# A DMA-bound 2x2 average pooling: loop bodies of two tiles and two result buffers instead of four, a split first load and a split last store

## The chip, the cores and the metric

One core of a Trainium2 chip. The time is the device time of one execution in microseconds (us); a kernel's figure is the median of several executions. A profiled execution also gives a span (first to last instruction), which in these runs is about 1.8 to 2.0 us shorter than the time of the same execution. The clock column is 1.000 and plays no part: there is no matrix work.

## The reference

```python
x = np.random.randn(32, 128, 256, 256).astype(np.float32)   # n, c, h, w
# kernel_size 2, stride 2
output[:, :, i, j] = np.mean(x[:, :, 2*i:2*i+2, 2*j:2*j+2], axis=(2, 3))
```

1073.74 MB are read and 268.44 MB are written, all in float32, with three additions and one multiplication for each result.

## The kernel before

A "unit" is 128 output rows, one for each partition. A tile has 32 units: 64 KB of input and 16 KB of output in each partition, so 8.39 MB in and 2.10 MB out. There are 127 whole tiles; the last 32 units go through in parts of 16, 8, 4 and 4 units, so that the end is short. SyncE (SP) issues the loads into two input buffers; VectorE (DVE) adds the two rows (first sum, in place) and then neighbouring columns (second sum, into a result buffer); ScalarE (ACT) multiplies by 0.25 and issues the store. SP, ACT and DVE synchronise by hand through semaphores; `take` waits for a semaphore and takes the count away again.

```python
OUTS = 4
ins = [in_pool.tile([P, TILE, 2 * w], f32, name="in_tile") for _ in range(2)]
res = [out_pool.tile([P, TILE, w_out], f32, name="res") for _ in range(OUTS)]

def tile_load(t, b):
    sp.dma_start(out=ins[b], in_=xt[t]).then_inc(loaded[b], 16)

def tile_sum(b, o, first=False):
    it, dst = ins[b], res[o]
    take(dve, loaded[b], 16)
    dve.tensor_add(out=it[:, :, 0:w], in0=it[:, :, 0:w], in1=it[:, :, w:]).then_inc(ready)
    if not first:
        take(dve, stored[o], 16)          # the result buffer's old store, between the sums
    take(dve, ready)
    dve.tensor_add(out=dst, in0=it[:, :, 0:w:2], in1=it[:, :, 1:w:2]).then_inc(summed)

def tile_scale(b, o, done):
    take(act, summed)
    act.sem_inc(free[b])                  # SP may now load into ins[b]
    act.mul(out=res[o], in_=res[o], mul=0.25).then_inc(done)
# ... (tile_store, the parts, the loops over OUTS tiles)
```

## Time and profile before

| | |
|---|---|
| median of 6 executions | 3103.94 us (3103.81 to 3104.12) |
| the profiled execution | 3104.85 us, span 3103.1 us |
| DVE busy, ACT busy | 54%, 15% |
| mean rate of the DMA engines | 433 GB/s |

The page of before: its first and second parts (busy us and share by engine; the span in 40 slices, where a digit is the busy share in tenths), then the DMA queues. Queue q1 holds the loads and q10 the stores; the last column is the time of their packets as a share of 16 DMA engines' span.

```profile
DVE 1679.7 (54%) x262; ACT 464.8 (15%) x132; POOL 0.2 (0%) x4
...
DMA  9999999999999999999999999999999999999999
...
q1 hardware_dynamic: 19008, 1075.85, 80.1%
q10 hardware_dynamic: 18720, 266.35, 20.0%
```

80.1 and 20.0 leave nothing: the DMA engines are the bound. The rhythm is in the timeline of before (columns: start us, length us, engine, line, operation, what it writes and reads, idle time before it and what ended it; SPq and ACTq lines are issues of DMAs by that engine's sequencer):

```profile
1495.40 8.69 DVE L88 TENSOR_TENSOR in_tile<-in_tile 128x8192 f32<-128x8192 f32 x1 [10.91 <-DVEq L70]
1504.24 4.42 DVE L92 TENSOR_TENSOR res<-in_tile 128x4096 f32<-128x4096 f32 x1
1508.86 3.62 ACT L97 ACTIVATE res<-res 128x4096 f32<-128x4096 f32 x1 [20.55 <-ACTq L70]
...
1512.72 0.34 ACTq L101 DMA_DIRECT2D out_dram<-res  x1
1519.59 8.69 DVE L88 TENSOR_TENSOR in_tile<-in_tile 128x8192 f32<-128x8192 f32 x1 [10.93 <-DVEq L70]
```

One tile every 24.18 us; the DVE works 13.1 us of it and waits 10.9 us. "DVEq L70" is the wait inside `take`; it does not tell which semaphore was waited for, so that has to be read from the moments at which DMAs land. The page's part on DMA issues gives the median time from issue to landing (last column):

```profile
out_dram<-res ACTq DMA_DIRECT2D x126, 2048.0 KB, 33.9
in_tile<-in_x_dram SPq DMA_DIRECT2D x127, 34.6
```

Each of these is longer than the 24.18 us period, so in both queues a DMA stands behind its predecessor. The records of single packets show how they share an engine: one 64 KB load packet (2.42 us), one 16 KB store packet (0.61 us), eight such pairs a tile. The chain of waits is of no use here: it ends after two pieces of 0.7 us at the last ScalarE instruction, because the DMAs behind it are not followed.

### The profile page before, as it was taken

What the parts mean: (1) busy time and instruction counts of PE and PEld (TensorE: products, weight loads), DVE (VectorE), ACT (ScalarE), POOL (GpSimd) and SP (SyncE); (2) the same over time, 40 slices, a digit from 0 to 9 for tenths busy, and PEclk for the clock granted to TensorE, in tenths of its full rate; (3) what the DMA queues carried; (4) which work ended last, traced back from release to release, by engine and by line L of the source; (5) the groups of instructions that cost most, each with busy time, mean ns of one, the idle gap of its engine ahead of it and who ended that gap; (6) DMA issues with size and microseconds to landing.
All of it is one profiled execution on the core that took longest, in us unless ns stands there. A gap on an engine that the chain in (4) does not pass through costs nothing. (4 is left out here: it accounts for less than half of the span.)

```text
span 3103.1 us, 2444 instructions
## 1 busy us (share of the span) xinstructions
DVE 1679.7 (54%) x262; ACT 464.8 (15%) x132; POOL 0.2 (0%) x4
## 2 busy tenths in 40 slices
DVE  4555555555555555555555555555555555555555
ACT  1111111111111111111111111111111111111111
POOL 0000000000000000000000000000000000000000
DMA  9999999999999999999999999999999999999999
GB/s 415 436 439 426 436 439 426 436 439 426 436 438 426 436 438 426 436 430 435 436 438 426 440 435 426 436 438 427 436 438 426 437 439 425 437 438 426 437 438 401
DMA packets 37730, 1342.21 MB, mean 433 GB/s; under 512 B 4192, under 2 KB 4192, under 8 KB 4576
## 3 DMA queue, kind: packets, MB, share of 16 engines
q1 hardware_dynamic: 19008, 1075.85, 80.1%
q10 hardware_dynamic: 18720, 266.35, 20.0%
q14 instruction: 2, 0.02, 0.0%
HBM read 1073.74 MB, written 268.44 MB: 433 GB/s over the span
## 5 line engine op out<-in xcount | busy, mean ns | idle before, releaser
L88 DVE TENSOR_TENSOR in_tile<-in_tile 128x8192 f32<-128x8192 f32 x127 | 1104.0, 8693 | 1395.9 <-DVEq L70 1395.9
L97 ACT ACTIVATE res<-res 128x4096 f32<-128x4096 f32 x127 | 459.2, 3616 | 2587.2 <-ACTq L70 2587.2
L92 DVE TENSOR_TENSOR res<-in_tile 128x4096 f32<-128x4096 f32 x127 | 562.0, 4425 | 18.6
L145 DVE TENSOR_TENSOR in_tile<-in_tile 128x1024 f32<-128x1024 f32 (+2 forms) x4 | 9.1, 2287 | 1.3 <-DVEq L70 1.3
L97 ACT ACT_TABLE_LOAD x1 | 1.3, 1283 | 36.5 <-ACTq L70 36.5
L164 ACT ACTIVATE res<-res 128x512 f32<-128x512 f32 (+2 forms) x4 | 4.2, 1056 | 8.4 <-ACTq L70 8.4
L147 DVE TENSOR_TENSOR res<-in_tile 128x512 f32<-128x512 f32 (+2 forms) x4 | 4.9, 1225 | 0.6
L249 POOL MEMSET const-bfloat16-1.0<- 128x1 bf16 x1 | 0.1, 101 | 0.0
L249 POOL MEMSET const-uint8-127<- 128x1 uint8 x1 | 0.1, 101 | 0.0
L249 POOL MEMSET const-float32-0.0<- 128x1 f32 x1 | 0.1, 98 | 0.2 <-issue 0.2
L249 POOL MEMSET const-float32-1.0<- 128x1 f32 x1 | 0.1, 98 | 0.0
## 6 DMA issues: line engine op xcount, KB each, us to landing
out_dram<-res ACTq DMA_DIRECT2D x126, 2048.0 KB, 33.9
in_tile<-in_x_dram SPq DMA_DIRECT2D x1, 4096.0 KB, 25.1
in_tile<-in_x_dram SPq DMA_DIRECT2D x1, 2048.0 KB, 30.2
in_tile<-in_x_dram SPq DMA_DIRECT2D x2, 1024.0 KB, 33.2
out_dram<-res SPq DMA_DIRECT2D x1, 2048.0 KB, 13.8
in_tile<-in_x_dram SPq DMA_DIRECT2D x127, 34.6
out_dram<-res ACTq DMA_DIRECT2D x1, 1024.0 KB, 7.4
out_dram<-res ACTq DMA_DIRECT2D x1, 512.0 KB, 5.4
```

The source lines that it names most:

```text
L88: dve.tensor_add(out=it[:, :, 0:w], in0=it[:, :, 0:w], in1=it[:, :, w:]).then_inc(ready)
L92: dve.tensor_add(out=dst, in0=it[:, :, 0:w:2], in1=it[:, :, 1:w:2]).then_inc(summed)
L97: act.mul(out=res[o], in_=res[o], mul=0.25).then_inc(done)
L145: dve.tensor_add(out=it[:, a:b, 0:w], in0=it[:, a:b, 0:w], in1=it[:, a:b, w:]).then_inc(ready)
L147: dve.tensor_add(out=dst[:, a:b], in0=it[:, a:b, 0:w:2], in1=it[:, a:b, 1:w:2]).then_inc(summed)
L164: act.mul(out=dst[:, a:b], in_=dst[:, a:b], mul=0.25).then_inc(scaled)
L249: nc = _bacc.Bacc("TRN2", target_bir_lowering=False, num_devices=1)
```

## The change

The intent: shorter programs (loop bodies of two tiles instead of four), result buffers in step with the two input buffers plus one for the last parts, an earlier start of the first load, and an earlier end of the last store. Core of the diff:

```diff
-    out_pool = ctx.enter_context(tc.tile_pool(name="outp", bufs=OUTS))      # OUTS = 4
+    out_pool = ctx.enter_context(tc.tile_pool(name="outp", bufs=3))
@@ first load
-        for b in range(2):
-            tile_load(b, b)
+        for p in (slice(0, P, 4), slice(1, P, 2), slice(2, P, 4)):
+            sp.dma_start(out=ins[0][p], in_=xt[0][p]).then_inc(first, 16)
+        load(1, 1)
@@ sums: the store's wait comes before the first sum now, and is for tile t-2
-        take(dve, loaded[b], 16)
-        dve.tensor_add(...).then_inc(ready)            # first sum
-        if not first:
-            take(dve, stored[o], 16)
-        take(dve, ready)
+    def tile_sums(b):
+        take(dve, stored[b], 16)
+        take(dve, loaded[b], 16)
+        sums(ins[b], res[b])                           # both sums
@@ DVE's start
+        for b in range(2):
+            dve.sem_inc(stored[b], 16)
+        take(dve, first, 48)
+        dve.sem_inc(loaded[0], 16)
@@ last 4 units
+                scale(dst[:, a:b], ended)
+                for k, engine in enumerate((act, sp)):
+                    engine.wait_ge(ended, 1)
+                    engine.dma_start(out=to[k::2], in_=dst[k::2, a:b]).then_inc(tail, 16)
# ... (loops, semaphores and names that follow from these are cut)
```

More of the change, by code (lines that the diff above doesn't have):

```diff
@@ L37 @@
 TILE = 32
-OUTS = 4
 def _pool_2x2(ctx, tc, x, out, units):
@@ L52, in _pool_2x2, with sem @@
     in_pool = ctx.enter_context(tc.tile_pool(name="inp", bufs=2))
-    out_pool = ctx.enter_context(tc.tile_pool(name="outp", bufs=OUTS))
+    out_pool = ctx.enter_context(tc.tile_pool(name="outp", bufs=3))
     ins = [in_pool.tile([P, TILE, 2 * w], f32, name="in_tile") for _ in range(2)]
-    res = [out_pool.tile([P, TILE, w_out], f32, name="res") for _ in range(OUTS)]
-    loaded = [ctx.enter_context(nc.semaphore(f"loaded{b}")) for b in range(2)]
-    free = [ctx.enter_context(nc.semaphore(f"free{b}")) for b in range(2)]
-    summed = ctx.enter_context(nc.semaphore("summed"))
-    scaled = ctx.enter_context(nc.semaphore("scaled"))
-    stored = [ctx.enter_context(nc.semaphore(f"stored{b}")) for b in range(OUTS)]
-    tail = ctx.enter_context(nc.semaphore("tail"))
-    ready = ctx.enter_context(nc.semaphore("ready"))
-    held = ctx.enter_context(nc.semaphore("held"))
+    res = [out_pool.tile([P, TILE, w_out], f32, name="res") for _ in range(3)]
+    def sem(name):
+        return ctx.enter_context(nc.semaphore(name))
+    first = sem("first")
+    loaded, free, stored = [[sem(f"{n}{b}") for b in range(2)] for n in ("loaded", "free", "stored")]
+    halfway, summed, scaled, held, ended, tail = [
+        sem(n) for n in ("halfway", "summed", "scaled", "held", "ended", "tail")
+    ]
     def take(engine, sem, n=1):
@@ L79, in _pool_2x2 @@
     ot = ov[0:whole * TILE * P].rearrange("(t p g) f -> t p g f", p=P, g=TILE)
-    loops, left = divmod(whole - OUTS, OUTS)
-    def tile_load(t, b):
-        sp.dma_start(out=ins[b], in_=xt[t]).then_inc(loaded[b], 16)
-    def tile_sum(b, o, first=False):
-        it, dst = ins[b], res[o]
-        take(dve, loaded[b], 16)
-        dve.tensor_add(out=it[:, :, 0:w], in0=it[:, :, 0:w], in1=it[:, :, w:]).then_inc(ready)
-        if not first:
-            take(dve, stored[o], 16)
-        take(dve, ready)
-        dve.tensor_add(out=dst, in0=it[:, :, 0:w:2], in1=it[:, :, 1:w:2]).then_inc(summed)
-    def tile_scale(b, o, done):
-        take(act, summed)
-        act.sem_inc(free[b])
-        act.mul(out=res[o], in_=res[o], mul=0.25).then_inc(done)
-    def tile_store(t, o):
-        take(act, scaled)
-        act.dma_start(out=ot[t], in_=res[o]).then_inc(stored[o], 16)
     parts, a = [], 0
@@ L105, in _pool_2x2, with load, sums @@
         b = rest if rest - a <= 4 else a + (rest - a) // 2
-        parts.append((a, b))
+        parts.append((a, b, sem(f"part{len(parts)}")))
         a = b
-    psem = [ctx.enter_context(nc.semaphore(f"part{k}")) for k in range(len(parts))]
-    with tc.tile_critical():
-        for b in range(2):
-            tile_load(b, b)
-        with sp.Fori(2, 2 + 2 * ((whole - 2) // 2), 2) as i:
+    def load(t, b):
+        sp.dma_start(out=ins[b], in_=xt[t]).then_inc(loaded[b], 16)
+    def sums(it, dst):
+        dve.tensor_add(out=it[:, :, 0:w], in0=it[:, :, 0:w], in1=it[:, :, w:]).then_inc(halfway)
+        take(dve, halfway)
+        dve.tensor_add(out=dst, in0=it[:, :, 0:w:2], in1=it[:, :, 1:w:2]).then_inc(summed)
@@ new lines, in tile_sums, with scale, scale_store @@
+    def tile_sums(b):
+        take(dve, stored[b], 16)
+        take(dve, loaded[b], 16)
+        sums(ins[b], res[b])
+    def scale(dst, done=scaled):
+        act.mul(out=dst, in_=dst, mul=0.25).then_inc(done)
+    def scale_store(t, b, landed):
+        take(act, summed)
+        act.sem_inc(free[b])
+        scale(res[b])
+        take(act, scaled)
+        act.dma_start(out=ot[t], in_=res[b]).then_inc(landed, 16)
+    with tc.tile_critical():
+        for p in (slice(0, P, 4), slice(1, P, 2), slice(2, P, 4)):
+            sp.dma_start(out=ins[0][p], in_=xt[0][p]).then_inc(first, 16)
+        load(1, 1)
+        pairs = (whole - 2) // 2
+        with sp.Fori(2, 2 + 2 * pairs, 2) as i:
@@ L116, in _pool_2x2 @@
             for b in range(2):
                 take(sp, free[b])
-                tile_load(i + b, b)
-        t = 2 + 2 * ((whole - 2) // 2)
-        while t < whole:
+                load(i + b, b)
+        for t in range(2 + 2 * pairs, whole):
             take(sp, free[t % 2])
-            tile_load(t, t % 2)
-            t += 1
+            load(t, t % 2)
         take(sp, free[whole % 2])
-        it, dst = ins[whole % 2], res[whole % OUTS]
-        for (a, b), s in zip(parts, psem):
-            sp.dma_start(out=it[:, a:b], in_=block((whole * TILE + a) * P, b - a)[0]).then_inc(s, 16)
+        it, dst = ins[whole % 2], res[2]
@@ L131, in _pool_2x2 @@
+        for a, b, part in parts:
+            sp.dma_start(out=it[:, a:b], in_=block((whole * TILE + a) * P, b - a)[0]).then_inc(part, 16)
         take(sp, held)
-        sp.dma_start(out=ot[whole - 1], in_=res[(whole - 1) % OUTS]).then_inc(stored[(whole - 1) % OUTS], 16)
-        for o in range(OUTS):
-            tile_sum(o % 2, o, first=True)
-        with dve.Fori(0, loops) as i:
-            for o in range(OUTS):
-                tile_sum(o % 2, o)
-        for o in range(left):
-            tile_sum(o % 2, o)
@@ L142, in _pool_2x2 @@
-        take(dve, stored[whole % OUTS], 16)
-        for (a, b), s in zip(parts, psem):
-            take(dve, s, 16)
-            dve.tensor_add(out=it[:, a:b, 0:w], in0=it[:, a:b, 0:w], in1=it[:, a:b, w:]).then_inc(ready)
-            take(dve, ready)
-            dve.tensor_add(out=dst[:, a:b], in0=it[:, a:b, 0:w:2], in1=it[:, a:b, 1:w:2]).then_inc(summed)
-        for t in range(OUTS):
-            tile_scale(t % 2, t, scaled)
-            tile_store(t, t)
-        with act.Fori(OUTS, OUTS + loops * OUTS, OUTS) as i:
-            for o in range(OUTS):
-                tile_scale(o % 2, o, scaled)
-                tile_store(i + o, o)
@@ L157, in _pool_2x2 @@
-        for t in range(OUTS + loops * OUTS, whole):
-            tile_scale(t % 2, t % OUTS, scaled if t < whole - 1 else held)
-            if t < whole - 1:
-                tile_store(t, t % OUTS)
-        act.sem_inc(free[(whole + 1) % 2], -1)
-        for a, b in parts:
-            take(act, summed)
-            act.mul(out=dst[:, a:b], in_=dst[:, a:b], mul=0.25).then_inc(scaled)
-            take(act, scaled)
-            act.dma_start(out=block((whole * TILE + a) * P, b - a)[1], in_=dst[:, a:b]).then_inc(tail, 16)
@@ L169, in _pool_2x2 @@
-        take(sp, tail, 16 * len(parts))
-        for o in range(OUTS):
-            if o != whole % OUTS:
-                take(sp, stored[o], 16)
+        sp.dma_start(out=ot[whole - 1], in_=res[(whole - 1) % 2]).then_inc(tail, 16)
+        for b in range(2):
+            dve.sem_inc(stored[b], 16)
+        take(dve, first, 48)
+        dve.sem_inc(loaded[0], 16)
+        with dve.Fori(0, whole // 2):
+            for b in range(2):
+                tile_sums(b)
+        if whole % 2:
+            tile_sums(0)
@@ new lines, in _pool_2x2 @@
+        for a, b, part in parts:
+            take(dve, part, 16)
+            sums(it[:, a:b], dst[:, a:b])
+        scale_store(0, 0, stored[0])
+        pairs = (whole - 3) // 2
+        with act.Fori(1, 1 + 2 * pairs, 2) as i:
+            for b in (1, 0):
+                scale_store(i + 1 - b, b, stored[b])
+        for t in range(1 + 2 * pairs, whole - 1):
+            scale_store(t, t % 2, stored[t % 2] if t < whole - 2 else tail)
+        take(act, summed)
+        scale(res[(whole - 1) % 2], held)
@@ new lines, in _pool_2x2 @@
+        for a, b, _ in parts:
+            take(act, summed)
+            to = block((whole * TILE + a) * P, b - a)[1]
+            if b < rest:
+                scale(dst[:, a:b])
+                take(act, scaled)
+                act.dma_start(out=to, in_=dst[:, a:b]).then_inc(tail, 16)
+            else:
+                scale(dst[:, a:b], ended)
+                for k, engine in enumerate((act, sp)):
+                    engine.wait_ge(ended, 1)
+                    engine.dma_start(out=to[k::2], in_=dst[k::2, a:b]).then_inc(tail, 16)
@@ L175, in _generic_pool @@
+        take(sp, tail, 16 * (len(parts) + 3))
+        sp.sem_inc(ended, -1)
 def _generic_pool(ctx, tc, x, out, k, s, n, c, h, w, h_out, w_out):
```

## The prediction

> **What bounds it now.** The DMA engines. The page's slices show them at least 90% busy in all 40; the load queue has 80.1%, the store queue 20.0% of 16 engines' span. In the timeline the first sums of consecutive tiles start every 24.18 us (1495.40, 1519.59). A tile moves 8.39 MB in and 2.10 MB out: 434 GB/s. The Trainium skill, "DMA: Bandwidth & Descriptors", section "Where 436 GB/s comes from", gives 435 as the ceiling; this trace agrees. Its section "Queues, rings and completion order" says each DMA engine takes its queues in turn by packet; the packet records agree: a 64 KB load packet (2.42 us), then a 16 KB store packet (0.61 us), eight pairs a tile, 24.2 us. VectorE is 54% busy (13.1 us a tile), ScalarE 15%: off the path until the tail. From the first packet (1.98 us) to the last the packet records show next to no idle, so three things can move: the head, one straggling DMA engine, the tail.
>
> The straggler: in the landings of every load from 66 us on, 15 engines finish within 0.6 us (66.19 to 66.82) and one 1.8 us later (68.59). It fell behind between 44 and 65 us, during the first store, and never catches up; most engines stop near 3099.2, the last at 3101.5.
>
> **What changes.**
> 1. Two result buffers instead of four, and the store of tile t-2 is awaited before tile t's first sum, not its second. In before, that store lands about 3.0 us after tile t's load (71.61 against 68.59). So each tile's sums start about 3 us later; the wait before them grows from 10.9 us once, but the period stays: the next load is now issued about 16.5 us after the last landing, and the DMA engines work on the load before it for 24.2 us. Some 4 to 8 us of slack remain. Steady state: 0 us.
> 2. First tile as 32+64+32 partitions, all still over 16 engines. In before the engines' first packets start over 1.98 to 2.96 us; a small first DMA should narrow that. Two more issues (0.33 us each) hide behind two packets of 2.4 us. Estimate: 0.3 us gained, up to 0.7. A different start might also spare the straggler: up to -1.8 us, chance about 40%.
> 3. Tail. With the straggler, the 3 us shift reaches tile 126: its sums end near 3083.6 instead of 3080.4; the parts then run back to back on VectorE, about 1.9 us later than before, so the last store is issued near 3098.9 instead of 3097.0, and DMA engines wait for it. Halving it over two queues shortens its start by an estimated 0.3 to 0.5 us (128 packets took 1 us to start on all engines). It lands near 3101.6, as before (3101.81). Without the straggler there is no shift and the end comes near 3100.
> 4. Shorter loops: fewer instructions, none on the path.
>
> **Prediction: 3102.8 us** (-0.03%), range 3099.8 to 3105.5. Faster by over 2%: 0.5%; within 2%: 99%; slower: 0.5%.
>
> **What would show it.** Period between first sums still 24.18 us; DMA 9 in all slices; the wait before a first sum ended by a store's landing, not a load's; first packets' starts less spread; the last landing's distance from the other 15 (1.8 us kept, or gone); last store issue at 3097 to 3099.
>
> **What would make it wrong.** If a load is issued after its predecessor has drained, DMA idles each tile: a period of 25 us costs 100 us (3%). If the split start makes more engines straggle, the end comes 2 to 4 us later.

## The result, and the profile after

| | before | after |
|---|---|---|
| median of 6 executions | 3103.94 us | 3104.09 us (3103.08 to 3104.27) |
| span of the profiled execution | 3103.1 us | 3102.3 us |
| ratio | | 1.0, 95% interval 0.9987 to 1.0013 |

A ratio is the mean time of one kernel's runs over that of the other's of the same rounds, so it is not quite the ratio of the medians quoted. The 0.8 us between the two spans is not a gain: the profiled execution of before took 3104.85 us, 0.9 us above its median.

The page after, the same parts:

```profile
DVE 1679.6 (54%) x262; ACT 464.7 (15%) x132; POOL 0.2 (0%) x4
...
DMA  9999999999999999999999999999999999999999
...
q1 hardware_dynamic: 19120, 1075.98, 80.1%
q10 hardware_dynamic: 18656, 266.22, 20.0%
```

The timeline of after:

```profile
1497.45 8.69 DVE L90 TENSOR_TENSOR in_tile<-in_tile 128x8192 f32<-128x8192 f32 x1 [10.91 <-DVEq L70]
1506.29 4.43 DVE L92 TENSOR_TENSOR res<-in_tile 128x4096 f32<-128x4096 f32 x1
1510.90 3.62 ACT L100 ACTIVATE res<-res 128x4096 f32<-128x4096 f32 x1 [20.56 <-ACTq L70]
...
1514.75 0.34 ACTq L107 DMA_DIRECT2D out_dram<-res  x1
1521.65 8.69 DVE L90 TENSOR_TENSOR in_tile<-in_tile 128x8192 f32<-128x8192 f32 x1 [10.94 <-DVEq L70]
```

And its DMA issues:

```profile
out_dram<-res ACTq DMA_DIRECT2D x126, 2048.0 KB, 30.8
in_tile<-in_x_dram SPq DMA_DIRECT2D x129, 31.5
```

The period is still 24.2 us and each wait is still 10.9 us long; only what ends it is another (a store's landing, not a load's). What moved is in the last two lines: loads and stores land 31.5 and 30.8 us after their issue instead of 34.6 and 33.9. They do not run faster. They are issued 3.1 us later in the same rhythm, because the sums of a tile begin when the store of the tile before last has landed. The start shows it: the third tile's load has landed at 66.80 us, the first tile's store at 69.77 us, and the third tile's first sum starts at 70.02 us (in before it started at 68.72 us, with its load landed at 68.59 us and the store at 71.61 us). The third tile's first sum in before:

```profile
68.72 8.69 DVE L88 TENSOR_TENSOR in_tile<-in_tile 128x8192 f32<-128x8192 f32 x1 [13.04 <-DVEq L70]
```

and in after, with the issue of the next load:

```profile
70.02 8.69 DVE L90 TENSOR_TENSOR in_tile<-in_tile 128x8192 f32<-128x8192 f32 x1 [14.06 <-DVEq L70]
...
83.63 0.33 SPq L87 DMA_DIRECT2D in_tile<-in_x_dram  x1
```

So the change spends 3 us of slack in each tile, and no time.

That left three questions: how much slack there was and is, what the head and the tail gained, and whether the change did anything to the one straggling DMA engine that the prediction read from the profile of before.

### The profile page after: what moved, and what is told of

Read it like the earlier page. It is cut to its first block, busy times and chain, and to the rows that moved or that the text cites. A ratio compares the mean times of both kernels' runs of the same rounds, so it can differ in the third digit from the quotient of the medians.

```text
span 3102.3 us, 2619 instructions
## 1 busy us (share of the span) xinstructions
DVE 1679.6 (54%) x262; ACT 464.7 (15%) x132; POOL 0.2 (0%) x4
## 5 line engine op out<-in xcount | busy, mean ns | idle before, releaser
L90 DVE TENSOR_TENSOR in_tile<-in_tile 128x8192 f32<-128x8192 f32 (+1 forms) x131 | 1113.1, 8497 | 1397.0 <-DVEq L70 1397.0
L100 ACT ACTIVATE res<-res 128x4096 f32<-128x4096 f32 (+1 forms) x131 | 463.5, 3538 | 2594.7 <-ACTq L70 2594.7
L92 DVE TENSOR_TENSOR res<-in_tile 128x4096 f32<-128x4096 f32 (+1 forms) x131 | 566.9, 4327 | 19.2
## 6 DMA issues: line engine op xcount, KB each, us to landing
out_dram<-res ACTq DMA_DIRECT2D x126, 2048.0 KB, 30.8
in_tile<-in_x_dram SPq DMA_DIRECT2D x129, 31.5
```

Of the source, the lines that this page charges most:

```text
L100: act.mul(out=dst, in_=dst, mul=0.25).then_inc(done)
```

## The experiments

Twelve kernels, each correct, in three groups, each run beside before on one chip (two chips in all). Times are medians; ratios are to runs of before on the same chip.

### Was the straggler the kernel's? (before_again, before_split_first, after_whole_first)

**before_again**: no edit.

> A control: the kernel before, unchanged. Theory (the straggling DMA engine comes from how the first tile's packets start, and is there in each execution): in every load from the third on one engine lands 1.5 to 2 us after the other 15. Rival (it is chance of one execution): the lag is another size here, or absent. Time 3103.8 to 3104.2 us.

Measured: 3104.08 us, before 3104.01 us in the same rounds; span 3102.2 us.

**before_split_first**: before with the first load of the changed kernel.

```diff
-        for b in range(2):
-            tile_load(b, b)
+        for p in (slice(0, P, 4), slice(1, P, 2), slice(2, P, 4)):
+            sp.dma_start(out=ins[0][p], in_=xt[0][p]).then_inc(first, 16)
+        tile_load(1, 1)
@@ DVE
+        take(dve, first, 48)
+        dve.sem_inc(loaded[0], 16)
```

> The kernel before with only the first load split in 32, 64 and 32 partitions. Theory (the split spares the straggler and costs at the head): the spread of the third load's landings falls from 2.4 us to under 0.6 us, the first sum starts at 23.5 to 23.8 us instead of 23.07, and the time is within 1 us of before. Rival (two buffers and the later sums removed the straggler): one engine is still 1.8 us late at the third load.

Measured: 3104.23 us, ratio 1.0 (0.9984 to 1.0017).

**after_whole_first**: the changed kernel with one DMA for the first tile.

```diff
-        for p in (slice(0, P, 4), slice(1, P, 2), slice(2, P, 4)):
-            sp.dma_start(out=ins[0][p], in_=xt[0][p]).then_inc(first, 16)
+        load(0, 0)
         load(1, 1)
-        take(dve, first, 48)
-        dve.sem_inc(loaded[0], 16)
```

> The changed kernel with the first tile loaded by one DMA again. Theory: the first sum starts at 23.0 to 23.2 us instead of 23.72, the first packets start over 1.98 to 2.96 us, and one engine lags by about 1.8 us from the third load on, which moves the tail by the 3 us wait: last store issued near 3098.5 us, end of the span 3102.5 to 3104. Rival (the lag comes from elsewhere): landings within 0.6 us and an end 0.3 us earlier than with the split.

Measured: 3103.43 us (3102.97 to 3103.84), ratio 0.9998 (0.9981 to 1.0014).

The head and the straggler in the landings and packet records of the profiled executions (us):

| kernel | first load | first packets of the 16 engines start | first tile landed | first sum starts | third load: 15th and last engine land | lag |
|---|---|---|---|---|---|---|
| before | whole | 1.98 to 2.96 | 22.93 | 23.07 | 66.82, 68.59 | 1.77 |
| before_again | whole | 2.00 to 2.53 | 22.82 | 22.96 | 66.50, 66.95 | 0.45 |
| after_whole_first | whole | 2.00 to 2.74 | 22.66 | 22.79 | 66.40, 66.44 | 0.04 |
| before_split_first | split | 2.33 to 3.28 | 23.07 | 23.41 | 66.95, 67.90 | 0.95 |
| after | split | 2.31 to 2.88 | 23.20 | 23.72 | 66.79, 66.80 | 0.01 |

The lag goes with neither the split nor the buffers: the very same kernel showed 1.77 us in one execution and 0.45 us in another, and a kernel with the whole first load had none. So the rivals of before_again and after_whole_first held, and before_split_first (0.95 us) lies between its two forecasts. It also comes later: in the profile of after it is 0.01 us at 66.8 us and 0.71 us at the load that landed at 1518.38 us. The theory that the start of the first tile makes it has fallen; the lag differs between executions of one kernel. What sets it off is open.

The split itself is a small loss. With it the first packets start 0.3 us later, not earlier: at 2.31 to 2.33 us in all eight profiled kernels that have it, against 1.97 to 2.00 us in the six that have not. The tile lands 0.1 to 0.5 us later, and the DVE, which now goes through three waits and adds to semaphores of its own, starts 0.34 to 0.52 us after the landing instead of 0.13 to 0.14 us. The time says nothing clear: without it 0.6 us less than before, far inside the interval.

### Is the last store's split worth anything? (after_one_last)

```diff
-                scale(dst[:, a:b], ended)
-                for k, engine in enumerate((act, sp)):
-                    engine.wait_ge(ended, 1)
-                    engine.dma_start(out=to[k::2], in_=dst[k::2, a:b]).then_inc(tail, 16)
+                scale(dst[:, a:b])
+                take(act, scaled)
+                act.dma_start(out=to, in_=dst[:, a:b]).then_inc(tail, 16)
```

> The changed kernel with the last store whole, on ScalarE's queue alone. Theory (the last store is backlogged behind the tail's other stores, so its start costs nothing): end of the span within 0.3 us of the changed kernel's. Rival (splitting saves part of the start-up): the end comes 0.3 to 0.7 us later.

Measured: 3104.00 us, ratio 1.0001 (0.9984 to 1.0018). The last landing is at 3101.13 us of the span, and with the split store at 3101.13 us too. The last store is queued behind those of the last whole tile and of the other parts, and their packets keep the engines busy from before its issue (3096.7 us) to 3099 us, when the first of them run out of work. The Trainium skill says of this, in "DMA: Bandwidth & Descriptors", section "Issuing engines are not separate DMA queues", that starting DMAs from several engines only saves the sequencer's issue time; this run agrees, and here even that (0.34 us an issue) was hidden.

### How much slack was there? (seven kernels with extra work)

If DMA sets the period, VectorE may be made slower without loss, until a load is issued too late. So the second sum was repeated in each whole tile, wholly or over part of the 32 units, which moves the release of the input buffer, the next load's issue and the store by the same time. In before:

```diff
         take(dve, ready)
+        for _ in range(1):                                # 2 in before_extra2
+            dve.tensor_add(out=dst, in0=it[:, :, 0:w:2], in1=it[:, :, 1:w:2]).then_inc(ready)
+            take(dve, ready)
         dve.tensor_add(out=dst, in0=it[:, :, 0:w:2], in1=it[:, :, 1:w:2]).then_inc(summed)
```

and the same between the sums of the changed kernel, where after_extra_half and after_extra_3q repeat 16 and 24 of the 32 units (`dst[:, :16]` and `it[:, :16, ...]`, or 24); before_extra1h repeats 32 and then 16. The parts of the tail are left as they are. The first four, in the order before_extra1, after_extra1, before_extra2, after_extra2:

> The kernel before with VectorE's second sum done twice in each whole tile, so that sums, next load and store all come about 4.6 us later after a load's landing. Theory (the period is set by the DMA engines' packets and all else has slack; a load is issued 10.7 us before the load ahead of it ends): 4.6 us less slack, period still 24.18 us, time 3104 to 3108 us. Rival (VectorE's time before the release counts): up to +4.6 us a tile, 3690 us.

> The changed kernel with the same 4.6 us. Theory (two result buffers leave a loop over two tiles: from the start of the sums to the store's issue 17.6 us, 4.6 us extra, about 1.3 us until its first packet, 24.2 us of alternating packets, 0.3 us: 48.0 us against 48.36 us of DMA work): just about flat, 3104 to 3120 us. Rival (the buffers play no part while DMA is full): the same as the kernel before with the same extra work, within 2 us.

> The kernel before with the second sum done three times in each tile: about 9.2 us later. Theory: the load's slack of 10.7 us is nearly used up but the four result buffers leave the stores theirs; period 24.2 to 24.5 us, 3104 to 3140 us.

> The changed kernel with the same 9.2 us. Theory (the loop through the two result buffers is now 52.6 us for two tiles): period up to 26.3 us, 3200 to 3370 us, with idle DMA engines or stores that wait, and the excess over the kernel before with the same extra work is what the third and fourth buffer were worth. Rival (the buffers play no part while DMA is full): the same as the kernel before with the same extra work.

Measured: before_extra1 is flat as expected. after_extra1 is 5.98% slower, so "just about flat" was wrong, and so was its rival. before_extra2 is 6.71% slower and after_extra2 12.26%; for before_extra2 I had expected at most some 1%, and after_extra2's 3487.67 us lies above the 3370 us expected at most.

The timeline of after_extra1, first sums only, shows the new rhythm:

```profile
1500.90 8.69 DVE L90 TENSOR_TENSOR in_tile<-in_tile 128x8192 f32<-128x8192 f32 x1 [13.62 <-DVEq L70]
...
1520.25 8.69 DVE L90 TENSOR_TENSOR in_tile<-in_tile 128x8192 f32<-128x8192 f32 x1 [1.51 <-DVEq L70]
...
1551.80 8.69 DVE L90 TENSOR_TENSOR in_tile<-in_tile 128x8192 f32<-128x8192 f32 x1 [13.72 <-DVEq L70]
```

Tiles come in pairs, 19.35 us and then 31.55 us apart: 50.9 us for two tiles instead of 48.4. The landings tell why. With the extra work the load of the fifth tile is issued at 92.87 us, when the load ahead of it has already begun to land (92.03 to 92.60 us). Without it the issue is at 83.63 us. It moved by 9.24 us for 4.57 us of work, so each us of lateness counted twice: the first tile's store comes later, which in the changed kernel holds up the third tile's first sum, and then the third tile's own sums are longer as well. From this came the theory of the next three runs, a limit of 2.9 us for the changed kernel and 8.9 us for before (in the order after_extra_half, after_extra_3q, before_extra1h):

> The changed kernel with the second sum repeated over half of each whole tile: about 2.45 us later. Theory (lateness counts twice: the first store comes later by it, so that the sums of the third tile start 3.2 us plus it after their load, and the next load's issue comes 13.5 us plus it after that; with about 1.3 us to the first packet the load queue runs dry when 18.0 us plus twice the extra work exceeds about 23.8 us, so at 2.9 us): flat, 3103 to 3107 us, the load of the fifth tile issued at about 88.5 us, before the landing of the fourth near 91.5 us. Rival (any lateness costs in the changed kernel, in proportion): about half of the 5.9% that 4.6 us cost, near 3195 us.

> The changed kernel with the second sum repeated over three quarters of each whole tile: about 3.5 us later. Theory (lateness counts twice, limit 2.9 us): over the limit, 3130 to 3270 us, with DMA engines that idle once in two tiles and sums that come in pairs 19.35 us apart. Rival (lateness counts once, limit 5.9 us, and something else slowed the kernel with 4.6 us): flat, under 3108 us.

> The kernel before with 7.0 us of extra work (the second sum repeated once whole and once over half of the tile). Theory (its sums wait for no store, lateness counts once: 13.5 us, the extra work and 1.3 us against 23.8 us, so the limit is 8.9 us): flat, 3104 to 3110 us. Rival (its limit is below that too, as 9.2 us cost 6.7%): 3150 us or more.

Measured: after_extra_half 0.95% slower (0.78 to 1.12), after_extra_3q 3.43%, before_extra1h 2.81%. For 2.44 us the issue moved by 5.42 us, to 89.05 us, about double, and the order held, but both limits were set too high. In after_extra_3q the issue moved by 9.64 us for 3.50 us, more than double: there one engine also landed the third load 1.98 us late. Its time lies in the range expected, but its rhythm does not stay as foretold: the first sums come in pairs at the start (76.16 and 95.52 us) and one by one, 24.7 to 25.3 us apart, at 1500 us, and its DMA engines idle for 8.8 us in the whole run.

### The wait's place or the number of buffers? (after_late_wait_extra1)

The changed kernel, two result buffers, extra work of 4.57 us, and only the store's wait moved to where before has it:

```diff
     def tile_sums(b):
-        take(dve, stored[b], 16)
         take(dve, loaded[b], 16)
-        sums(ins[b], res[b], extra=1)
+        sums(ins[b], res[b], extra=1, gate=stored[b])
@@ sums, after the first tensor_add
+        if gate is not None:
+            take(dve, gate, 16)
         take(dve, halfway)
```

> The changed kernel, still with two result buffers, with the 4.6 us of extra work, and the wait for the store moved back between the two sums, where the kernel before has it. Theory (the place of the wait costs the slack, not the number of buffers: the store lands about 6 to 8 us after the load, when the first sum of 8.8 us is still running): flat, 3104 to 3108 us, as the kernel before with the same extra work. Rival (two buffers are too few for the late store): as slow as with the early wait, near 3287 us, or between.

Measured: 3106.02 us, ratio 1.0006 (0.9989 to 1.0023), against 1.0598 with the early wait. Its timeline:

```profile
1495.20 8.69 DVE L90 TENSOR_TENSOR in_tile<-in_tile 128x8192 f32<-128x8192 f32 x1 [6.36 <-DVEq L70]
1504.04 4.43 DVE L95 TENSOR_TENSOR res<-in_tile 128x4096 f32<-128x4096 f32 x1
1508.61 4.42 DVE L97 TENSOR_TENSOR res<-in_tile 128x4096 f32<-128x4096 f32 x1
...
1519.38 8.69 DVE L90 TENSOR_TENSOR in_tile<-in_tile 128x8192 f32<-128x8192 f32 x1 [6.34 <-DVEq L70]
```

The period is 24.18 us again, and between the first sum and the next pass there is no wait at all (1495.20 + 8.69 is 1503.89, the next begins at 1504.04): the store, which lands 6.0 us after the load (74.42 against 68.38 us), is there before the first sum of 8.7 us is done. So with two result buffers the early wait takes the slack, and with the late wait two are as good as before's four up to 4.57 us of extra work (3106.02 and 3105.57 us). Four buffers with the early wait were not run. The landings of before suggest that this would be free too: the wait would be for the store of tile t-4, and the first tile's store landed at 71.61 us, the fifth tile's load at 116.95 us. So the loss needs both, the early wait and only two buffers; that second half is argued and not shown.

### All of them together

"Lead" is how long before the first of 16 engines finishes the fourth tile's load the fifth tile's load is issued, in the profiled execution. "Lead later" is the median of the same for the 13th to the 122nd load; where loads differ in turn, the medians of both kinds. The last two columns, from the packet records, are sums over the run for one DMA engine, in the mean of the 16: how much longer than 2.42 us its load packets were, and how long it had no packet (start-up and end left out; good to about 1 us).

| kernel | extra work, us | median us | ratio | issue, us | first landing, us | lead, us | lead later, us | longer load packets, us | idle, us |
|---|---|---|---|---|---|---|---|---|---|
| before_again | 0 | 3104.08 | 1.0 | 80.70 | 90.26 | 9.6 | 9.4 | 0.6 | 0.0 |
| before_extra1 | 4.57 | 3105.57 | 1.0006 | 85.71 | 91.12 | 5.4 | 5.2 | 1.1 | 1.4 |
| before_extra1h | 7.02 | 3193.52 | 1.0281 | 92.45 | 93.77 | 1.3 | 1.3 | 92.0 | 7.2 |
| before_extra2 | 9.15 | 3311.19 | 1.0671 | 96.60 | 96.16 | -0.4 | 0.0 | 168.0 | 35.7 |
| after | 0 | 3104.09 | 1.0 | 83.63 | 90.59 | 7.0 | 6.2 | 0.5 | 0.0 |
| after_extra_half | 2.44 | 3132.53 | 1.0095 | 89.05 | 90.00 | 0.9 | 2.7 | 28.5 | 1.6 |
| after_extra_3q | 3.50 | 3202.44 | 1.0343 | 93.27 | 91.07 | -2.2 | 2.2 | 81.5 | 8.8 |
| after_extra1 | 4.57 | 3286.58 | 1.0598 | 92.87 | 92.03 | -0.8 | -0.8, 6.5 | 97.9 | 74.3 |
| after_extra2 | 9.15 | 3487.67 | 1.1226 | 99.64 | 97.28 | -2.4 | -2.4, 3.5 | 97 | 287 |
| after_late_wait_extra1 | 4.57 | 3106.02 | 1.0006 | 86.69 | 91.94 | 5.2 | 5.2 | 1.2 | 1.9 |

A lead of 5.2 us or more costs at most 2 us in all; with 2.7 us or less later in the run the kernel pays. The fifth tile's lead alone misleads: after_extra_half starts with 0.9 us and settles at 2.7 us, and pays all along. Between 2.7 and 5.2 us nothing was run. The last two columns account for the whole loss: before_extra1h's 92.0 + 7.2 us stand against a span longer by 98.6 us than before_again's (3200.8 less 3102.2), and after_extra1's 97.9 + 74.3 us against 171.3 us over after (3273.6 less 3102.3).

One warning lies in it. before_extra1h loses 2.8% though its DMA engines are hardly ever idle. Here are stretches of 1000 us of it (columns: busy us of the engines, granted clock, DMA share, GB/s):

```profile
1000.00:2000.00 1000.00, 796.64 (x162) 144.64 (x40) 0.00 (x0) 1.00 1.00 421
2000.00:3000.00 1000.00, 796.16 (x161) 144.65 (x40) 0.00 (x0) 1.00 1.00 421
```

and the same stretches of after:

```profile
1000.00:2000.00 1000.00, 540.41 (x83) 151.88 (x42) 0.00 (x0) 1.00 1.00 434
2000.00:3000.00 1000.00, 540.87 (x83) 148.26 (x41) 0.00 (x0) 1.00 1.00 434
```

The DMA share is 1.00 in all four, and only the rate tells: 421 instead of 434 GB/s. The time went into packets that took longer: 5766 of the 16256 whole load packets took over 2.48 us, against 64 in after. The long packets are not the ones that start a load: counted by the order of their starts within each load, from the sixth tile on, the first of an engine's eight packets took 0.03 us over 2.42 us on average, the third and the fourth 0.25 us. Nor is it the added work as such: before_extra1 has 67 long packets with more of it than after_extra_half, which has 2253. Why they take longer was not tested.

## Why the prediction was right

The time, 3104.09 us, lies within the predicted range (3099.8 to 3105.5) and 1.3 us above the point.

- **The bound** was right: 434 GB/s and DMA 9 in all slices in both kernels. The extra work shows it directly: 4.57 us more VectorE work in each of 127 tiles, 580 us in all, cost before 1.7 us.
- **Steady state, "0 us"** was right, with the mechanism as told: sums about 3 us later (70.02 us against a load landed at 66.80 us), released by the store (landed at 69.77 us), period unchanged. The next load's issue came 16.8 us after the last landing (83.63 less 66.80); the prediction said 16.5. The phrase that the wait grows "from 10.9 us once" held too (14.06 us before the third tile, then 10.9).
- **"Some 4 to 8 us of slack remain"** was mis-sized as a margin. The lead of a load is 7.0 us at the start and 6.2 us later, but extra work of 2.44 us already cost 0.95%. Lateness counts twice in the changed kernel at the start, and in after_extra_half loads that were issued 2.7 us ahead of the landing were not free. The prediction counted lateness once and asked for no lead.
- **The head, "0.3 us gained, up to 0.7"**, failed in sign. The spread of the first packets was narrower in after than in before (0.57 us instead of 0.98), but that is chance: over the profiled kernels it is 0.53 to 0.98 us without the split and 0.45 to 1.29 us with it. All of them started later (from 2.31 us), and the first sum started at 23.72 us instead of 22.8 to 23.1. after_whole_first and before_split_first show that the split is the cause.
- **The straggler** was read rightly from the trace and wrongly explained. "Might spare the straggler" gave the split a power that it does not have: before_again shows the same kernel with a lag of 0.45 us. Part of the foreseen gain was therefore no gain to be had: the profile of before fell on an execution 0.9 us above the median.
- **The tail**: "without the straggler there is no shift" was not put to the test, as a lag was there again: 0.98 us when the store that frees the last whole tile's buffer landed (3068.02 us). The tile's sums started at 3068.27 us, 2.1 us later than in before_again (3066.19 us), whose lag there was 0.67 us; the parts' sums then ran without a wait, the last store was issued at 3096.60 us instead of 3095.95 us, and the last landing came at 3101.13 us instead of 3100.96 us. So the shift came, smaller than foretold, and hardly moved the end. "Halving it over two queues shortens its start by an estimated 0.3 to 0.5 us" failed: after_one_last ends at the same 3101.13 us, because that store is queued behind others in any case.

So the right time came from the one step that mattered (a later release hidden by a queue that is still full) and from small terms of the head and tail that could not add up to much. The foreseen gain of 1.1 us (3103.94 less 3102.8) is about the head's 0.3 us and the straggler's 1.8 us at a chance of 40%, the two terms that failed. That the time stayed in the range although they failed is luck, in so far as both are small.

Nothing here beats both kernels clearly. after_whole_first has the lowest median (3103.43 us), but before's 3104.01 us of the same rounds lies inside its interval. If the changed kernel is kept, the wait between the sums is the better place for it: it was tried only with the extra work, and there it took away the whole loss.

## What to carry to other kernels

Where queues are always full, ask of a change not whether an engine now waits but how far ahead of need the next transfer is still issued; that lead is the margin, and a change can spend it without showing in the time. To see it, add dummy work to the engine that releases the buffers and find where the time begins to rise. Put a wait for a buffer directly in front of the first instruction that writes it, not in front of work that could cover it.

## What the Trainium skill lacked or had wrong

- "DMA: Bandwidth & Descriptors", "Queues, rings and completion order": the turn-taking of queues by packets agrees with the trace (2.42 us load, 0.61 us store, in turn). It lacks that loads issued with too little lead can cost rate while the engines stay busy: 421 GB/s instead of 434 at a DMA share of 1.00, with a third of the load packets over 2.48 us.
- The same page, "Latency and other measured facts", gives about 600 ns to the first byte for DMAs of SyncE and ScalarE. Here the first packet of the first load started 1.02 us after its issue began (0.96 to 1.98 us), the last engine's 2.0 us after, and with the split first load none before 1.35 us (0.96 to 2.31 us). The trace shows packets and not bytes, so the two are not quite the same thing.
- No page that I read says that the lag of one of the 16 DMA engines behind the other 15 differs between executions of the same kernel: 0.45 us and 1.77 us at the third load in two of them. It can stay (before: 1.78 us at the load that landed at 3067.05 us) or go (after_extra_3q: 1.98 us at the third load, 0.06 us at the fifth).
